# A page softmax in fewer steps through PSUM, and the substitution steps of a delta net on GpSimd: a hybrid decoder step on one NeuronCore

## The chip, the cores and the metric

The kernel runs on one core of a Trainium2 chip. Its time is the device time of one execution in microseconds (us), and a kernel's time is the median of its runs. The engines are TensorE (PE in the profile; its weight loads are PEld), VectorE (DVE), ScalarE (ACT), GpSimd (POOL) and SyncE (SP), which issues most of the DMAs. Each engine carries out its own instructions in a fixed order; semaphores make it wait for others.

## What is computed

One inference step of a hybrid decoder layer: a prompt of 1024 tokens and a sample group of 8 requests with one token each. One input projection feeds three groups of heads (differential attention, Mamba-2 SSD, gated delta net) and their gates; a projection of the concatenated heads closes the layer. Two parts matter here.

The sample group's attention reads 32 pages of 128 cached keys for each of its 8 requests, adds the new token itself, and takes a softmax over all of them for each of 4 heads x 2 maps, of which the second is subtracted with a weight lam:

```python
logits = jnp.einsum('bqhmd,bkhmd->bmhqk', q, k) * (DH_A ** -0.5)
logits = logits + rel_pos_bias(q_pos, k_pos, table)
p = jax.nn.softmax(logits, axis=-1)
wts = p[:, 0] - lam * p[:, 1]
return jnp.einsum('bhqk,bkhd->bqhd', wts, v)
```

The gated delta net solves, for each head and each chunk of 64 tokens, a unit lower triangular system, and then runs a chain over 16 chunks:

```python
lower = jnp.where(strict, beta[..., :, None] * kk * decay, 0.0)
sol = lax.linalg.triangular_solve(lower + eye, rhs, left_side=True, lower=True, unit_diagonal=True)
u, w = sol[..., :DV_C], sol[..., DV_C:]
...
S1, o = lax.scan(step, S0, seq_in)
```

## The kernel before

From about 70 to 850 us, TensorE works on the input projection (`proj_fm`, matmuls on line L458). Each weight tile is cut into a high half by ACT (`whi`, L155) and a low half by GpSimd (`wlo`, L201), and three products per pair are summed, so a late `wlo` stops TensorE. Three sets of these halves are in flight. Results leave through DVE: the convolution of a column group is one product and three multiply-adds into `cy` (L971, L167). The projections are cut into four segments (`CUTS = (9, 18, 30, 33)`), and beside each segment the function `drive` takes turns among three generators: the projections, the delta-net heads (`gdn_all`, four heads one after the other) and the sample group's pages (`sample_attention`). The kernel is built with a scheduler that simulates its own timeline and from this settles the order in which each engine gets its instructions. A segment's projections, its share of the heads and its share of the pages are all placed before the next segment's projections begin.

`sample_attention` goes over the requests. For each pair of key pages (`k_pages`) GpSimd multiplies the pages by the query in four products (`kt`, L842) and DVE sums them into the logits `lg` (L843). Behind a request's last pair comes `page_softmax`: the maximum over the pages on DVE (`smx`), a transpose on TensorE (L853) and a second maximum to join the partitions, a diagonal matrix of it (`sdg`, L857) spread by a matmul (L858), subtraction, exponentials on ACT, sums (`ssm`, matmul at L870), a reciprocal, and the weights `wz`. The new token's own logits, `slfb`, go the same way apart from the pages (`ses`, `wself`). The weights multiply the value pages on TensorE (`pv`, L898) while the next request's keys come in.

`gdn_head` handles one head of the delta net. It builds the triangular blocks of 32 rows, writes them to DRAM (`invd`) and reads them back as `Dm`, with one block on each partition. 31 substitution steps then invert all blocks at once:

```python
for j in range(31):
    n, m = 31 - j, j // 4 + 1
    tv = U[:, 8:16].rearrange("p a b -> p (a b)")[:, 0:m * n].rearrange("p (c i) -> p c i", i=n)
    tt(tv, bl(U[:, 0:m, j], n), bm(Dm[:, j, j + 1:32], m), ALU.mult)
    step = tt(U[:, 0:m, j + 1:32], U[:, 0:m, j + 1:32], tv, ALU.subtract)
    gstep[:] = [step.ins]
```

`bl` and `bm` repeat an operand over an axis; `tt` runs on DVE and shows as line L159, `tte("g", ...)` runs on GpSimd and shows as L164. These are 62 instructions a head, each on the result of the one ahead of it, with m*n elements per partition (8 to 76). The result goes through `invd` once more (L1151, L1154, issued by ACT) into `LT`, TensorE transposes it (L1163), and small matmuls join the blocks and run the chunks. Beside the steps `kb` (DVE) and `kN` (GpSimd, L1157) are scaled. `behind_gdn` puts the products or sums of `k_pages` that run on the steps' engine behind the last step written so far.

From 850 to about 1105 us the prompt's attention, the SSD, head 3 of the delta net and the last pages run; the output projection (L1833) closes the kernel.

Of the kernel before, what the change touches and what calls it, by code (L numbers as in the profile page):

```python
# [9 lines left out]
F32 = mybir.dt.float32  # L10
# [3 lines left out]
AF = mybir.ActivationFunctionType  # L14
# [5 lines left out]
P = 128  # L20
# [6 lines left out]
NPG = 32  # L27
# [51 lines left out]
def bl(ap, n):  # L79
    return ap.unsqueeze(len(ap.shape)).broadcast_to(list(ap.shape) + [n])  # L80


def bm(ap, n):
    return ap.unsqueeze(1).broadcast_to([ap.shape[0], n] + list(ap.shape[1:]))
# [3 lines left out]
def trunk_kernel(  # L88
# [61 lines left out]
    def small(shape, n, dt=F32, bufs=2):  # L150
        return sp.tile(shape, dt, tag=n, name=nm(n), bufs=bufs)

    def act(out, in_, func, bias=0.0, scale=1.0, accum=None):
        if accum is None:
            return S.activation(out, in_, func, bias=bias, scale=scale)  # L155
        return S.activation(out, in_, func, bias=bias, scale=scale, accum_out=accum)  # L156

    def tt(out, a, b, op):
        return V.tensor_tensor(out=out, in0=a, in1=b, op=op)  # L159
# [6 lines left out]
    def stt(out, a, s, b, op0, op1):  # L166
        return V.scalar_tensor_tensor(out=out, in0=a, scalar=s, in1=b, op0=op0, op1=op1)  # L167
# [601 lines left out]
        yield NT, 3.4  # L769


    lsg = const.tile([P, 4, 2], F32, name="lsg")
    G.memset(lsg, 1.0)
    slfb = const.tile([P, NS, 8], F32, name="slfb")
    wself = const.tile([P, NS, 4], F32, name="wself")
    wz = const.tile([P, NPG, 32], F32, name="wz")
# [58 lines left out]
    def k_pages(b, qb, lg, g):  # L835
        kt = kvp.tile([P, 2, 512], F32, tag="kt", name=nm("kt"), bufs=KB)
        for j in range(2):
            page(cache_k, b * NPG + 2 * g + j, kt[:, j, :])
        with behind_gdn():
            for j in range(2):  # L840
                for c in (slice(0, 256), slice(256, 512)):
                    G.tensor_tensor(out=kt[:, j, c], in0=kt[:, j, c], in1=qb[:, c], op=ALU.mult)  # L842
            V.tensor_reduce(out=lg[:, 2 * g:2 * g + 2, :], in_=kt.rearrange("p j (a d) -> p j a d", d=64), axis=AX.X, op=ALU.add)  # L843

    def page_softmax(b, lg):
        l31 = lg[:, NPG - 1, :].rearrange("p (h m) -> p h m", m=2)
        tt(l31, l31, bl(fb, 2), ALU.add)
        mx = small([P, 8], "smx")
        V.tensor_reduce(out=mx, in_=lg.rearrange("p g a -> p a g"), axis=AX.X, op=ALU.max)
        tt(mx, mx, slfb[:, b, :], ALU.max)  # L850

        pt = bank()
        TE.transpose(pt[0:8, 0:P], mx, ident)  # L853
        m8 = small([8, 1], "sm8")
        V.tensor_reduce(out=m8, in_=pt[0:8, 0:P], axis=AX.X, op=ALU.max)
        dg = small([8, 8], "sdg")
        V.tensor_scalar_mul(dg, ident[0:8, 0:8], m8)  # L857
        TE.matmul(pt[:, 256:264], ones[0:8, :], dg, start=True, stop=True)  # L858
        pmx = small([P, 8], "spm")
        V.tensor_copy(pmx, pt[:, 256:264])  # L860
        tt(lg, lg, bm(pmx, NPG), ALU.subtract)
        act(lg, lg, AF.Exp)
        es = small([P, 8], "ses")
        tt(es, slfb[:, b, :], pmx, ALU.subtract)
        act(es, es, AF.Exp)
        sm = small([P, 8], "ssm")
        V.tensor_reduce(out=sm, in_=lg.rearrange("p g a -> p a g"), axis=AX.X, op=ALU.add)
        tot = small([P, 8], "sto")
        pt = bank()
        TE.matmul(pt[:, 0:8], ones, sm, start=True, stop=True)  # L870
        tt(tot, pt[:, 0:8], es, ALU.add)
        V.reciprocal(tot, tot)
        tt(tot, tot, lsg.rearrange("p h m -> p (h m)"), ALU.mult)
        tt(lg, lg, bm(tot, NPG), ALU.mult)
        l4 = lg.rearrange("p g (h m) -> p g h m", m=2)
        if b > 0:
            G.memset(wz[:, :, 4 * b - 4:4 * b], 0.0)
        tt(wz[:, :, 4 * b:4 * b + 4], l4[:, :, :, 0], l4[:, :, :, 1], ALU.add)
        tt(es, es, tot, ALU.mult)
        e2 = es.rearrange("p (h m) -> p h m", m=2)  # L880
        tt(wself[:, b, :], e2[:, :, 0], e2[:, :, 1], ALU.add)

    vq = []

# [20 lines left out]
    def sample_attention():  # L905
        for b in range(NS + 1):
            if b < NS:
                qb = half(n="qb")
                SP.dma_start(out=qb, in_=qd[b:b + 1, :].broadcast_to([P, 512]))
                lg = small([P, NPG, 8], "lg")  # L910
            vg = 0
            for g in range(NPG // 2):
                if b < NS:
                    k_pages(b, qb, lg, g)
                    yield 2.4
                if b > 0:
                    want = 16 if b == NS else max(0, g - 2) * 16 // 13 + 1
                    while vg < min(16, g + VB if b == NS else want + 1):
                        if len(vq) == VB:
                            v_mul()  # L920
                            yield 1.0
                        v_load(b - 1, vg)
                        vg += 1
                    while len(vq) > 1 and vg - len(vq) + 1 < want and g > 2:
                        v_mul()
                        yield 1.0
            while vq:
                v_mul()
                yield 1.0
            if b < NS:  # L930
                page_softmax(b, lg)
                yield 4.0
        wd = small([NS, NS, 4], "wd", bufs=1)
        tt(wd, wself[0:NS], bl(ident[0:NS, 0:NS], 4), ALU.mult)
        TE.matmul(pv[0:32, :], wd, vS, start=False, stop=True)
        hm = small([P, 4], "hm", bufs=1)
        V.tensor_reduce(out=hm, in_=ident.rearrange("p (a h) -> p h a", h=4), axis=AX.X, op=ALU.add)
        sb = small([P, NS], "sb", bufs=1)
        V.tensor_reduce(out=sb, in_=ident.rearrange("p (j b h) -> p b j h", b=NS, h=4), axis=AX.XY, op=ALU.add)
        pvs = half(n="pvs")  # L940
        tt(pvs.rearrange("p (h d) -> p h d", d=P), pv.rearrange("p (h d) -> p h d", d=P), bl(hm, P), ALU.mult)
        pst = bank()
        TE.matmul(pst[0:NS, :], sb, pvs, start=True, stop=True)
        oS = half([NS, 512], n="oS")
        S.copy(oS, pst[0:NS, :])
        finish_sample(oS, 0)
        yield 1.0
# [94 lines left out]
    def gdn_head(h):  # L1042
# [100 lines left out]
        for j in range(31):  # L1143
            n, m = 31 - j, j // 4 + 1
            tv = U[:, 8:16].rearrange("p a b -> p (a b)")[:, 0:m * n].rearrange("p (c i) -> p c i", i=n)
            tt(tv, bl(U[:, 0:m, j], n), bm(Dm[:, j, j + 1:32], m), ALU.mult)
            step = tt(U[:, 0:m, j + 1:32], U[:, 0:m, j + 1:32], tv, ALU.subtract)
            gstep[:] = [step.ins]
            yield 0.5
        for g in range(4):  # L1150
# [533 lines left out]
    fb = const.tile([P, 4], F32, name="fb")  # L1684
    V.tensor_copy(fb, pst[:, 0:4])

    V.tensor_copy(lsg[:, :, 1], nlam.broadcast_to([P, 4]))

    sample_q()
    smp = sample_attention()  # L1690
    drive((chain(items(1), small_cols()), 52.0), (take(smp, 16 * 2.4 - 0.1), 40.0))
# [252 lines left out]
```

## Time and profile before

| | before |
|---|---|
| runs, us | 1272.66, 1275.63, 1278.05; median 1275.63 |
| profiled execution, us | 1270.58, span 1268.8 |
| TensorE busy | 1136.3 us, mean granted clock 0.947 of full speed |
| DVE busy | 833.6 us |
| GpSimd busy | 643.8 us |
| ACT busy | 471.6 us |

The span is the time from the first to the last instruction in the trace of the profiled execution. The share of busy time is a mean over stretches that have different limits; what ends an engine's idle time in a stretch is read from the waits and the rows in time. The granted clock is 1 at 2.4 GHz and 0.5 at 1.2 GHz.

### The profile page before, as it was taken

How to read it: one execution, taken by the hardware profiler on the slowest of the kernel's cores; microseconds unless marked ns; L12 is line 12 of the kernel's file. 1: busy time of each engine (PE TensorE's matmuls, PEld its weight loads, DVE VectorE, ACT ScalarE, POOL GpSimd, SP SyncE). 2: the span in 40 equal slices, each digit the busy share in tenths (PEclk: the TensorE clock that was granted, in tenths of full speed). 3: DMA queues.
4: the chain of work that ended last, by engine and by line, in shares of the span. 5: the costliest groups of instructions: out<-in, count | busy, mean ns of one | idle time of the engine just before them, and what ended most of it. 6: DMA issues, size and time to landing. Idle time of an engine off the chain costs nothing.

```text
span 1268.8 us, 22346 instructions
## 1 busy us (share of the span) xinstructions
PE 1136.3 (90%) x7365; PEld 959.4 (76%) x7365; DVE 833.6 (66%) x1994; ACT 471.6 (37%) x998; POOL 643.8 (51%) x779
## 2 busy tenths in 40 slices
PE   4999999989889988888997799988899999799997
PEld 3799887768669777867866688866568778678876
DVE  6723698549478658945754955787878988664444
ACT  6332223211114332233353233436737759341111
POOL 3747867646665653573965778772023251341100
PEclk9999999989789988898988899998998999899999
DMA  8646765994884962696797599999786664961420
GB/s 298 200 164 205 238 208 161 349 324 134 280 293 155 319 214 77 190 333 211 234 318 226 183 322 336 307 287 257 219 225 174 161 167 133 299 198 52 131 69 34
DMA packets 246452, 275.57 MB, mean 217 GB/s; under 512 B 31905, under 2 KB 163376, under 8 KB 246322
## 3 DMA queue, kind: packets, MB, share of 16 engines
q1 hardware_dynamic: 168082, 214.44, 52.3%
q10 hardware_dynamic: 78256, 59.72, 16.4%
q8 instruction: 58, 0.95, 0.3%
q14 instruction: 56, 0.46, 0.1%
HBM read 231.59 MB, written 42.67 MB: 216 GB/s over the span
## 4 chain that ended last, share of the span: by engine, by line
PE 53%; DMA 16%; DVE 15%; issue 5%; ACT 3%; SPq 3%; POOL 3%; ACTq 1%; DVEq 0%; POOLq 0%
PE b L458 23%; PE b L1833 10%; PE pv L898 4%; DMA kt<-in_cache_k_dram 3%; DVE U L159 3%; DMA vt<-in_cache_v_dram 3%; DMA w<-in_w_in_dram 2%; DVE lg L843 2%; DVE cy L167 2%; PE b L745 1%; SPq L823 1%; POOL kt L842 1%; PE b L1893 1%; DVE e L721 1%; DMA zb<-zfd 1%
## 5 line engine op out<-in xcount | busy, mean ns | idle before, releaser
L458 PE MATMUL b<-hh,whi 128*128 128x344 f32 (+1 forms) x2016 | 508.6, 335 | 23.0 <-DVE cy L167 11.6
L842 POOL TENSOR_TENSOR kt<-kt,qb 128x256 f32<-128x256 f32 x512 | 364.5, 745 | 159.8 <-DMA kt<-in_cache_k_dram 104.0
L458 PEld LDWEIGHTS b<-hh,whi 128*128 128x128 f32 x2016 | 363.7, 197 | 56.0 <-issue 30.1
L458 PE MATMUL b<-hh,wlo 128*128 128x344 f32 (+1 forms) x1008 | 332.4, 334 | 3.5 <-POOL wlo L201 3.5
L843 DVE TENSOR_REDUCE lg<-kt 128x16 f32<-128x1024 f32 x128 | 154.6, 1211 | 88.0 <-POOL kt L842 85.2
L458 PEld LDWEIGHTS b<-hh,wlo 128*128 128x128 f32 x1008 | 197.1, 196 | 15.7 <-issue 10.1
L201 POOL TENSOR_TENSOR wlo<-w,whi 128x512 fp32r<-128x512 f32 x86 | 111.1, 1297 | 92.9 <-ACT whi L155 80.5
L1833 PE MATMUL b<-wo,mh 128*128 128x512 f32 (+1 forms) x408 | 121.7, 380 | 0.2 <-POOL wo L1567 0.2
L155 ACT ACTIVATE whi<-w 128x512 fp32r<-128x512 f32 x86 | 54.1, 631 | 160.8 <-PE b L458 114.4
L167 DVE SCALAR_TENSOR_TENSOR cy<-b,vec,cy 128x341 f32<-128x341 f32 (+4 forms) x180 | 99.0, 563 | 1.5 <-DVE U L159 0.2
L898 PE MATMUL pv<-vt,wz 128*32 128x512 f32 x512 | 78.3, 645 | 22.6 <-DMA vt<-in_cache_v_dram 15.0
L1833 PEld LDWEIGHTS b<-wo,mh 128*128 128x128 f32 x408 | 74.6, 188 | 14.5 <-POOL wo L1567 0.4
L1833 PE MATMUL b<-wo,ml 128*128 128x512 f32 (+1 forms) x204 | 77.1, 378 | 0.0
L1801 POOL TENSOR_TENSOR ml<-zt,mh 128x512 fp32r<-128x512 f32 x16 | 22.4, 1404 | 104.7 <-ACT mh L1800 104.5
L159 DVE TENSOR_TENSOR U<-U,Dm 128x60 f32<-128x60 f32 (+24 forms) x124 | 40.6, 327 | 18.7 <-DMA Dm<-invd 16.8
L156 ACT ACTIVATE e<-e,nmx 128x128 f32<-128x128 f32 (+7 forms) x64 | 48.9, 766 | 8.8 <-DVE nmx L723 5.4
L155 ACT ACT_TABLE_LOAD x33 | 42.3, 1283 | 25.5 <-DMA qh<-qfd 8.5
L718 PE MATMUL b<-kTh,qh 128*128 128x128 f32 (+3 forms) x96 | 41.1, 431 | 11.7 <-DVE mx L721 6.5
L159 DVE TENSOR_TENSOR y<-b,gate 128x512 f32<-128x512 f32 (+1 forms) x17 | 11.1, 658 | 54.2 <-PE b L1833 54.2
L1833 PEld LDWEIGHTS b<-wo,ml 128*128 128x128 f32 x204 | 38.3, 188 | 7.3
L971 DVE TENSOR_SCALAR cy<-b,vec 128x344 f32<-128x344 f32 (+1 forms) x60 | 33.2, 564 | 14.5 <-PE b L458 14.3
L898 PEld LDWEIGHTS pv<-vt,wz 128*32 128x32 f32 x512 | 12.4, 110 | 39.6 <-issue 18.9
(531 smaller groups left out, 2022.9 us busy)
## 6 DMA issues: line engine op xcount, KB each, us to landing
kt<-in_cache_k_dram SPq DMA_DIRECT2D x256, 256.0 KB
vt<-in_cache_v_dram SPq DMA_DIRECT2D x256, 256.0 KB
w<-in_w_in_dram ACTq DMA_DIRECT2D x82, 256.0 KB
zfd<-zf ACTq DMA_DIRECT2D x12, 512.0 KB
wo<-in_w_out_dram SPq DMA_DIRECT2D x12, 512.0 KB
om<-mixd SPq DMA_DIRECT2D x24, 256.0 KB
xt<-in_x_prompt_dram SPq DMA_DIRECT2D x8, 512.0 KB
hx<-in_w_ada_dram SPq DMA_DIRECT2D x16, 256.0 KB
```

The costliest lines, as they stand in the source:

```text
L155: return S.activation(out, in_, func, bias=bias, scale=scale)
L156: return S.activation(out, in_, func, bias=bias, scale=scale, accum_out=accum)
L159: return V.tensor_tensor(out=out, in0=a, in1=b, op=op)
L167: return V.scalar_tensor_tensor(out=out, in0=a, scalar=s, in1=b, op0=op0, op1=op1)
L201: G.tensor_tensor(out=lo, in0=w32, in1=hi.bitcast(F32), op=ALU.subtract)
L458: TE.matmul(ps[:, 0:N], a, b[k][:, sl], start=(i == 0), stop=(i == 23))
L718: TE.matmul(ps[:, 0:b - a], qh[:, m, ts], kT[m][:, a:b], start=True, stop=False)
L842: G.tensor_tensor(out=kt[:, j, c], in0=kt[:, j, c], in1=qb[:, c], op=ALU.mult)
L843: V.tensor_reduce(out=lg[:, 2 * g:2 * g + 2, :], in_=kt.rearrange("p j (a d) -> p j a d", d=64), axis=AX.X, op=ALU.add)
L898: mm = TE.matmul(pv[32 * r:32 * r + 32, :], wz[:, 2 * g + j, :], vt[:, j, :], start=(b == 0 and g < 2), stop=(b == NS - 1 and g >= 14 and ...
L971: V.tensor_scalar_mul(y[:, c0_:c0_ + m], ps[:, o:o + m], wv[3])
L1833: TE.matmul(ps[c], m[a][:, kt % 4, :], w[kt][:, c[0]:c[1]], start=(kt == KT[0] and i == 0), stop=(kt == KT[-1] and i == 2))
```

## The change

Two parts. In `page_softmax` the new token's logits become row 32 of `lg`, copied there by ACT, so that maximum, exponential, normalisation and the subtraction of the second map handle pages and new token together. The diagonal matrix, the copy of the spread maximum out of PSUM and the separate steps on `ses` go; DVE reads the spread maximum and the reciprocal from PSUM directly, and the factor -lam moves into the last two instructions, so `lsg` goes too. The pairs of key pages are visited in the order 14, 15, 0, 1, ..., 13, and the bias of the last page is added behind the second pair. In `gdn_head` the 62 substitution steps of a head move from DVE to GpSimd. `behind_gdn` then orders GpSimd's `kt` products behind the steps, where it ordered DVE's sums.

```diff
     def page_softmax(b, lg):
-        l31 = lg[:, NPG - 1, :].rearrange("p (h m) -> p h m", m=2)
-        tt(l31, l31, bl(fb, 2), ALU.add)
+
+        if b == 0:
+            S.copy(lg[:, NPG, :], slfb[:, b, :])
         mx = small([P, 8], "smx")
         V.tensor_reduce(out=mx, in_=lg.rearrange("p g a -> p a g"), axis=AX.X, op=ALU.max)
-        tt(mx, mx, slfb[:, b, :], ALU.max)
...
-        dg = small([8, 8], "sdg")
-        V.tensor_scalar_mul(dg, ident[0:8, 0:8], m8)
-        TE.matmul(pt[:, 256:264], ones[0:8, :], dg, start=True, stop=True)
-        pmx = small([P, 8], "spm")
-        V.tensor_copy(pmx, pt[:, 256:264])
-        tt(lg, lg, bm(pmx, NPG), ALU.subtract)
+        TE.matmul(pt[:, 256:264], m8.broadcast_to([8, P]), ident[0:8, 0:8], start=True, stop=True)
+        tt(lg, lg, bm(pt[:, 256:264], NPG + 1), ALU.subtract)
         act(lg, lg, AF.Exp)
-        es = small([P, 8], "ses")
-        tt(es, slfb[:, b, :], pmx, ALU.subtract)
-        act(es, es, AF.Exp)
         sm = small([P, 8], "ssm")
-        V.tensor_reduce(out=sm, in_=lg.rearrange("p g a -> p a g"), axis=AX.X, op=ALU.add)
-        tot = small([P, 8], "sto")
+        V.tensor_reduce(out=sm, in_=lg[:, 0:NPG].rearrange("p g a -> p a g"), axis=AX.X, op=ALU.add)
         pt = bank()
         TE.matmul(pt[:, 0:8], ones, sm, start=True, stop=True)
-        tt(tot, pt[:, 0:8], es, ALU.add)
-        V.reciprocal(tot, tot)
-        tt(tot, tot, lsg.rearrange("p h m -> p (h m)"), ALU.mult)
-        tt(lg, lg, bm(tot, NPG), ALU.mult)
+        tot = small([P, 8], "sto")
+        tt(tot, pt[:, 0:8], lg[:, NPG, :], ALU.add)
+        V.reciprocal(pt[:, 8:16], tot)
+        tt(lg, lg, bm(pt[:, 8:16], NPG + 1), ALU.mult)
...
-        tt(wz[:, :, 4 * b:4 * b + 4], l4[:, :, :, 0], l4[:, :, :, 1], ALU.add)
-        tt(es, es, tot, ALU.mult)
-        e2 = es.rearrange("p (h m) -> p h m", m=2)
-        tt(wself[:, b, :], e2[:, :, 0], e2[:, :, 1], ALU.add)
+        stt(wz[:, :, 4 * b:4 * b + 4], l4[:, 0:NPG, :, 1], nlam, l4[:, 0:NPG, :, 0], ALU.mult, ALU.add)
+        stt(wself[:, b, :], l4[:, NPG, :, 1], nlam, l4[:, NPG, :, 0], ALU.mult, ALU.add)
...
-                    k_pages(b, qb, lg, g)
+                    k_pages(b, qb, lg, (g - 2) % (NPG // 2))
+                    if g == 1:
+                        l31 = lg[:, NPG - 1, :].rearrange("p (h m) -> p h m", m=2)
+                        tt(l31, l31, bl(fb, 2), ALU.add)
...
-            tt(tv, bl(U[:, 0:m, j], n), bm(Dm[:, j, j + 1:32], m), ALU.mult)
-            step = tt(U[:, 0:m, j + 1:32], U[:, 0:m, j + 1:32], tv, ALU.subtract)
+            tte("g", tv, bl(U[:, 0:m, j], n), bm(Dm[:, j, j + 1:32], m), ALU.mult)
+            step = tte("g", U[:, 0:m, j + 1:32], U[:, 0:m, j + 1:32], tv, ALU.subtract)
```

Lines behind the diff have numbers lower by 7 in the kernel of the change (L1163 is L1156 there, L1151 is L1144, L1157 is L1150), L842 is L840 and L898 is L886. The order of the instructions changes with it. Two places follow.

First place: GpSimd, in the substitution steps of head 0. Before, GpSimd has here weight splits (`wlo`), page products (`kt`) and `kN`:

```order
L201 TENSOR_TENSOR wlo_3659<-w_473_3624,whi_3658 128x512
L842 TENSOR_TENSOR kt_3439<-kt_3439,qb_3265 128x256 x4
L201 TENSOR_TENSOR wlo_3746<-w_474_3626,whi_3745 128x512
L842 TENSOR_TENSOR kt_3500<-kt_3500,qb_3265 128x256 x4
L201 TENSOR_TENSOR wlo_3912<-w_502_3877,whi_3911 128x512
```

With the change the steps (`U_2827`; the ones with `Dm` are the products, the others the differences) stand among them, here near their end:

```order
L201 TENSOR_TENSOR wlo_3727<-w_468_3607,whi_3726 128x512
L164 TENSOR_TENSOR U_2827<-U_2827 128x6x8
L201 TENSOR_TENSOR wlo_3893<-w_496_3858,whi_3892 128x512
L164 TENSOR_TENSOR U_2827<-U_2827,Dm_2822 128x49
L164 TENSOR_TENSOR U_2827<-U_2827 128x7x7
L164 TENSOR_TENSOR U_2827<-U_2827,Dm_2822 128x42
L164 TENSOR_TENSOR U_2827<-U_2827 128x7x6
L164 TENSOR_TENSOR U_2827<-U_2827,Dm_2822 128x35
L164 TENSOR_TENSOR U_2827<-U_2827 128x7x5
L840 TENSOR_TENSOR kt_3337<-kt_3337,qb_3244 128x256 x4
L164 TENSOR_TENSOR U_2827<-U_2827,Dm_2822 128x28
```

The split `wlo_3893` is the last one ahead of the end of head 0's steps; 15 steps and 4 `kt` products stand behind it up to the last step.

Second place: TensorE, at the transpose of head 2's `LT`. Before, it stands among the projections of the segment that ends at item 30 (`b`, L458), with 68 of them still to come:

```order
L458 MATMUL b_8566<-hh_514,wlo_8393 128x344
L458 MATMUL b_8566<-hh_525,whi_8392 128x344
L1163 MATMUL b_8155<-ident,LT_7281 128x128 x4
L1163 MATMUL b_8163<-ident,LT_7281 128x128 x4
L898 MATMUL pv<-vt_8396,wz 32x512 x2
L898 MATMUL pv<-vt_8408,wz 32x512 x2
L458 MATMUL b_8566<-hh_526,whi_8392 128x344
L458 MATMUL b_8566<-hh_525,wlo_8393 128x344
```

With the change:

```order
L458 MATMUL b_8666<-hh_772,whi_8422 128x344
L458 MATMUL b_8666<-hh_771,wlo_8423 128x344
L886 MATMUL pv<-vt_8021,wz 32x512 x2
L886 MATMUL pv<-vt_8089,wz 32x512 x2
L886 MATMUL pv<-vt_8167,wz 32x512 x2
L886 MATMUL pv<-vt_8283,wz 32x512 x2
L1156 MATMUL b_8100<-ident,LT_7235 128x128 x4
L1156 MATMUL b_8108<-ident,LT_7235 128x128 x4
L1168 MATMUL b_8147<-T_958_7426,LT_7235 32x32 x4
L1169 MATMUL b_8148<-T_958_7426,LT_7235 32x32 x4
```

The transpose moved behind the last projection of its segment (`b_8666`). Between the segment's last projection and the next segment's first one stand 104 other matmuls, those on pages (`pv`) included; before there were 36.

## Rows read from the trace of the kernel before

**Rows 1.** The page, part 1: busy us, share of span, instructions.
```profile
PE 1136.3 (90%) x7365; PEld 959.4 (76%) x7365; DVE 833.6 (66%) x1994; ACT 471.6 (37%) x998; POOL 643.8 (51%) x779
```

**Rows 2.** TensorE's waits: line, releaser, us in total, times, longest.
```profile
PE b L858 <- DVE sdg L857: 4.1, 2, 3.6
PE pv L898 <- DVE wz L159: 4.0, 2, 2.8
...
PE b L458 <- POOL wlo L201: 3.5, 3, 2.7
```

**Rows 3.** TensorE in time, four windows: start, us, instruction, [idle before].
```profile
482.23 0.94 PE L458 MATMUL b<-hh,whi 128*128 128x344 f32 x2 [6.14 <-DVE cy L167]
...
700.24 0.27 PE L853 MATMUL b<-ident,smx 128*8 128x128 f32 x1 [2.02 <-DVE U L159]
...
709.59 0.59 PE L858 MATMUL b<-sdg,ones 8*128 8x8 f32 x2 [3.62 <-DVE sdg L857]
...
727.45 1.08 PE L898 MATMUL pv<-vt,wz 128*32 128x512 f32 x8 [2.78 <-DVE wz L159]
```

**Rows 4.** Windows: busy us of PE, PEld, DVE, ACT, POOL; PEclk; DMA.
```profile
559.50:578.90 19.40, 13.81 (x106) 8.90 (x105) 13.56 (x23) 3.57 (x7) 16.07 (x23) 0.89 0.95 312
688.00:731.40 43.40, 34.99 (x189) 33.29 (x188) 41.43 (x98) 10.64 (x17) 27.94 (x33) 0.85 0.56 178
731.40:766.30 34.90, 34.90 (x303) 29.91 (x301) 14.19 (x16) 13.53 (x26) 26.27 (x33) 0.99 0.98 321
...
900.00:940.00 40.00, 35.44 (x242) 22.39 (x242) 34.29 (x162) 16.35 (x47) 4.54 (x8) 1.00 0.82 241
```

**Rows 5.** Windows of instructions on tile U: DVE busy, POOL busy, PEclk, DMA.
```profile
276.00:321.40 45.40, 17.61 (x62) 0.00 (x0) 1.00 0.64 201
...
688.00:731.40 43.40, 25.82 (x62) 0.00 (x0) 0.85 0.56 178
...
900.00:940.00 40.00, 14.78 (x62) 0.00 (x0) 1.00 0.82 241
```

**Rows 6.** Rows in time on TensorE at the ends of two segments.
```profile
334.20 1.06 PE L1163 MATMUL b<-ident,LT 128*128 128x128 f32 x8 [1.83 <-DMA LT<-invd]
...
774.10 0.56 PE L458 MATMUL b<-hh,whi 128*128 128x344 f32 x2
...
775.13 0.48 PE L458 MATMUL b<-hh,whi 128*128 128x344 f32 x2
```

**Rows 7.** GpSimd by line and form: busy us, mean ns, idle before.
```profile
L842 POOL TENSOR_TENSOR kt<-kt,qb 128x256 f32<-128x256 f32 x512 | 364.5, 745 | 159.8 <-DMA kt<-in_cache_k_dram 104.0 <-DVE U L159 12.8 <-DMA qb<-qd 10.7
L201 POOL TENSOR_TENSOR wlo<-w,whi 128x512 fp32r<-128x512 f32 x86 | 111.1, 1297 | 92.9 <-ACT whi L155 80.5 <-PE b L1119 9.7 <-PE b L458 1.4
...
L164 POOL TENSOR_TENSOR stm<-sst,sbc 128x256 f32<-128x256 f32 x8 | 7.8, 994 | 6.4 <-DVE sst L159 6.4
L1157 POOL TENSOR_TENSOR kN<-kN,fkd 128x1024 f32<-128x1024 f32 x4 | 7.6, 1897 | 10.9 <-DVE kb L159 10.9
```

**Rows 8.** Rows in time on GpSimd: a memset and the copies behind it.
```profile
946.51 0.31 POOL L1497 MEMSET gwz<- 128x256 f32 x1 [2.11 <-PE b L1501]
946.88 0.33 POOL L1499 COPY gwz<-gWQ 128x8 f32<-128x8 f32 x2
```

**Rows 9.** Rows in time: steps on DVE alone, then beside GpSimd's kt products.
```profile
483.33 0.19 DVE L159 TENSOR_TENSOR U<-U,Dm 128x30 f32<-128x30 f32 x1
483.56 0.19 DVE L159 TENSOR_TENSOR U<-U 128x30 f32<-128x30 f32 x1
...
698.67 3.54 POOL L842 TENSOR_TENSOR kt<-kt,qb 128x256 f32<-128x256 f32 x5 [3.06 <-DMA qb<-qd]
...
700.26 0.64 DVE L159 TENSOR_TENSOR U<-U,Dm 128x63 f32<-128x63 f32 x1
```

**Rows 10.** Tile U: count, ns min/median/max, first and last start.
```profile
L159 DVE TENSOR_TENSOR U<-U,Dm x124: 156/211/1826, 276.2 to 938.9; 128x60 f32<-128x60 f32 x12, 128x28 f32<-128x28 f32 x8, 128x54 f32<-128x54 f32 x8, 128x48 f32<-128x48 f32 x8
```

**Rows 11.** DVE by line and form: a product that GpSimd runs too.
```profile
L164 DVE TENSOR_TENSOR stm<-sst,sbc 128x256 f32<-128x256 f32 x8 | 6.0, 766 | 0.0
```

More of the change, by code (lines that the diff above doesn't have):

```diff
@@ L769, in attn_head @@
         yield NT, 3.4
-    lsg = const.tile([P, 4, 2], F32, name="lsg")
-    G.memset(lsg, 1.0)
     slfb = const.tile([P, NS, 8], F32, name="slfb")
@@ L909, in sample_attention @@
                 SP.dma_start(out=qb, in_=qd[b:b + 1, :].broadcast_to([P, 512]))
-                lg = small([P, NPG, 8], "lg")
+                lg = small([P, NPG + 1, 8], "lg")
+                if b > 0:
+                    S.copy(lg[:, NPG, :], slfb[:, b, :])
             vg = 0
@@ L1685, in trunk_kernel @@
     V.tensor_copy(fb, pst[:, 0:4])
-    V.tensor_copy(lsg[:, :, 1], nlam.broadcast_to([P, 4]))
     sample_q()
```

## The prediction

> **What bounds the kernel now.** I read the page's shares of the engines first: TensorE is busy for 90% of the span, DVE for 66%, GpSimd for 51% [rows 1]. So the change pays only where TensorE waits for DVE, and costs only where TensorE comes to wait for GpSimd. Next come TensorE's own waits. The page softmax's maximum (sdg) and weights (wz) hold it for 4.1 and 4.0 us in two places each [rows 2]. The rows in time show the largest of these, and a wait of the softmax's transpose, within one stretch: 2.02, 3.62 and 2.78 us [rows 3]. It is the stretch in which the third delta-net head (head 2) runs its 62 substitution steps on DVE. DVE is busy there for 41.43 of 43.40 us, and TensorE's mean granted clock is 0.85 [rows 4]. With the two levels of 2.4 and 1.2 GHz that is 30% of the stretch at the lower one, so some 6.5 us of matmul time went with the clock, and 8.4 us with the three waits. A fourth wait, of 6.14 us, stands at the start of head 1's steps and ends with a convolution sink on DVE [rows 3].
>
> Each head is also a chain: 62 dependent steps, two trips through DRAM (invd, LT), a transpose on TensorE (L1163), and a row of small matmuls behind it. The windows over tile U give the steps 17.61, 25.82 and 14.78 us of DVE at heads 0, 2 and 3, inside stretches of 45, 43 and 40 us [rows 5]. Where a segment's projections run out, TensorE has little besides this chain. At head 0 it waited 1.83 us until LT had landed at 334.20 [rows 6], 12.8 us after the steps' end near 321.4. At head 1 the last part of the delta net took 19.4 us, with TensorE busy for 13.81 [rows 4]. Head 2 escaped that: projections go on at 774.10 [rows 6], behind a part in which TensorE was never idle (731.4 to 766.3, rows 4).
>
> **The price of a step on GpSimd.** The trace of before has no U step there. The nearest rows are products and differences of two f32 operands: 745 ns at 256 elements, 1297 ns at 512 [rows 7]. The line through them is 193 ns + 2.16 ns an element. A head's 31 products and 31 differences have 1560 elements each (the sum of m*n in the code), so 62 x 0.193 + 3120 x 0.00216 = 18.7 us. Each step also waits for the one ahead of it: a GpSimd copy that needs a memset starts at 946.88, the memset ends at 946.51 + 0.31 [rows 8], so 60 ns, 3.7 us a head. Together **22.4 us a head, 0.36 us a step**. On DVE a step of 30 elements takes 0.19 us and the next starts 0.23 us after it, but 0.64 us beside GpSimd's kt products [rows 9]; that is how head 2 came to its 25.82 us. My lower bound is DVE's undisturbed pace, 62 x 0.23 = 14.3 us. The upper is 0.5 us a step, twice the foot of the line with its wait (2 x 0.253), 31 us. I take the line, since 8 to 76 elements lie near its foot.
>
> That DVE's steps grow beside kt products is what the Trainium skill ("SBUF — State Buffer", Who interferes with whom) has for a DVE instruction with two SBUF inputs against a GpSimd instruction that reads SBUF: one blocks the other for a whole instruction. The trace agrees, 0.64 against 0.19 us. By that rule the moved steps would go on holding up DVE's two-input work, for a third of a microsecond at a time.
>
> **Part by part.**
> - *Softmax.* DVE loses some ten short instructions per sample, eight times. TensorE's waits for sdg, wz and the transpose are about 10 us, 8.4 of them in head 2's stretch, which has its own term. Elsewhere **-2** (0 to -5). ACT gains a copy of 8 elements per sample, at a use of 37% [rows 1]; I cost it at nothing, because ACT cuts weights several matmuls ahead of their use, and where that lead is gone it costs its own 0.2 us, eight times.
> - *Head 0.* In the order of the change GpSimd has 62 steps, 16 kt products, 6 weight splits and kN in one row: 22.4 + 16 x 0.745 + 6 x 1.297 + 1.9 = 44.0 us. From 276.2 that ends at 320.2, as before, if nothing waits. But the last split (wlo_3893) stands ahead of the last 15 steps and 4 kt products, and 54 projection matmuls ahead of the segment's end. At about 0.17 us each (six in 1.03 us, rows 6) with some page matmuls between them that is near 321. Then 1.3 + 15 x 0.3 + 3.0 us put the chain's end near 329, and LT at 341 against 334.2, or 3 us sooner where the split's high half is ready sooner: **+5** (-1.6 to +10).
> - *Head 1.* Sinks no longer queue with steps, so the wait of 6.14 us and the half clock behind it should shrink. The steps still start when Dm has landed. **-3** (0 to -8).
> - *Head 2.* The largest term. In the order of before the transpose stands 68 projections ahead of the segment's end; in the order of the change it stands behind all of them, and 104 other matmuls, those on pages included, are left with no projection among them, where it was 36. GpSimd's row within the chain is 62 steps, 20 kt products, 8 splits, 12 products of the sample state (at most 0.994 us each) and kN: 22.4 + 14.9 + 10.4 + 11.9 + 1.9 = 61.5 us [rows 7]. From 688.1 that is 749.6; the trips, 12 to 12.8 us as at head 0, bring 762. The serial part takes at least the 19.4 us that head 1's took, so projections resume near 783 against 774.10: **+9**. TensorE's vanished waits (8.4 + 6.5 us) and the moved matmuls bring it to the segment's end sooner, near 740, and are swallowed by the wait for LT. Low, at DVE's pace: 688.1 + 14.3 + 39.1 + 12 + 19.4 = 772.9, -1. High, at 0.5 us a step: 758 + 12.8 + 22 = 793, +19.
> - *Head 3.* GpSimd is nearly empty there (4.54 us of 40), DVE has 34.29, TensorE 35.44 [rows 4]. 14.78 us leave DVE, and TensorE's 4.6 us of idle time bound the gain: **-3** (0 to -4.6). The chain itself, 22.4 us with little between its steps, fits its old 40 us.
> - *Given back.* Where TensorE is later, page transfers are further ahead of it: **-2**.
>
> Sum: -2 + 5 - 3 + 9 - 3 - 2 = +4 us. The profiled execution took 1270.58 us (span 1268.8), 5 us less than the median of the three runs, so 1274.6 for such an execution and **1279.5 us** for a median of runs. A measurement tells 0.5%, 6.4 us, from no change; +4 is inside that. By itself this case spans 1269 to 1282.
>
> **The rivals.**
> - *The relief comes through: faster, 1257.* If steps cost DVE's pace on GpSimd, or fill the time in which GpSimd waited for kt pages (104 us in all, rows 7), heads 0 and 2 give -1.6 and -1, head 1 -8, softmax -5, head 3 -3: -19 us. For it: DVE's 41.43 of 43.40 us, and GpSimd at 26.27 of 34.9 us beside a TensorE that never idles [rows 4]. Against: 61 us of work in one row ahead of head 2's transpose. It decides where a step costs under 0.27 us.
> - *Late weight splits: slower, 1294.* Twenty splits now queue among steps and kt products. In the order of before the first matmul on such a split stands 14 to 60 projections behind it; in that of the change, five have 7 to 11, or 1.2 to 1.9 us. If GpSimd lags the planned order by more, TensorE stalls by the lag: at 0.46 us a step 62 x 0.1 = 6 us a head, over three heads +18. Against: TensorE waited for splits for 3.5 us in all [rows 2], and the planned spacing of 2.4 to 2.75 projections a step, 0.41 to 0.47 us, is wider than my price. It decides from about 0.45 us a step.
> - *Steps at twice DVE's duration: slower, 1288.* DVE's products of a step have a median of 211 ns [rows 10]. Twice that, 62 x 0.422 = 26.2 us a head, is 4 us over my price, and heads 0 and 2 both end that much later: +8. The Trainium skill ("GPSIMD Engine Reference", Engine selection) has GpSimd about twice as slow for elementwise work on two inputs. This trace shows 994 ns on GpSimd [rows 7] against 766 ns on DVE [rows 11] for the same 256-element product, a ratio of 1.3, so it bears the rule out only in part.
> - *Hidden anyway.* Both parts concern engines off the path and the transposes come in time: 1272 to 1276, within the likeliest case's span.
>
> **How the numbers follow.** No measurable change 0.37, relief 0.27, late splits 0.20, twice the duration 0.12, slower in other ways 0.04: faster 0.27, same 0.37, slower 0.36. The range runs from the relief's 1257, less 1 us, to the late splits' 1294 plus 3; it leaves out about half of the first and a third of the second.
>
> **What would show it.** Right: U steps on GpSimd near 0.30 us with gaps near 60 ns; hardly any idle time on GpSimd from head 2's first step to its last; L1156 of head 2 waiting for LT, projections resuming near 783; head 0's LT near 340; no softmax wait of TensorE over 1 us elsewhere. Wrong: steps under 0.25 or over 0.43 us, TensorE waiting for wlo by over 10 us in sum, or head 2's LT landing before TensorE reaches the segment's end.

## The result, and the profile after

The change makes the kernel slower: a median of 1292.93 us (1290.80 to 1297.42, 4 runs) against 1276.84 us (4 runs), a ratio of 1.0139 with a 95% interval of 1.0103 to 1.0174. The profiled execution, of 1297.42 us, is the slowest of the four, so some 4 us of its span are not in the median. Where runs of one kernel lie over 1.5% above its fastest, as two of the four of experiment 7 do, they are given apart and no median is taken over them.

The engines' shares in the page of the change, beside [rows 1]:

```profile
PE 1150.5 (89%) x7365; PEld 969.4 (75%) x7365; DVE 765.3 (59%) x1697; ACT 477.0 (37%) x1002; POOL 712.0 (55%) x1026
```

DVE has 68 us less to do, GpSimd 68 us more, and TensorE's share falls by a point. TensorE's waits in the change (line, releaser, us in total, times, longest), beside [rows 2]:

```profile
PE pv L886 <- DMA vt<-in_cache_v_dram: 21.0, 8, 8.7
PE b L1218 <- ACT oC L155: 11.1, 3, 5.6
PE b L458 <- POOL wlo L201: 9.6, 4, 3.8
...
PE b L458 <- DVE cy L167: 6.7, 4, 3.0
...
PE b L1156 <- DMA LT<-invd: 5.4, 2, 4.9
...
PE pv L886 <- DVE wz L167: 0.4, 1, 0.4
```

Of the softmax's waits of 4.1 and 4.0 us (for `sdg` and `wz`) 0.4 us are left. In their place stand longer waits for value pages (21.0 us against 15.0 before, among them one of 8.7), for the chunk chain of the delta net (11.1, `oC`) and for `LT` (5.4). The waits for splits are 9.6 us against 3.5.

The substitution steps, beside [rows 10] and [rows 5], first their durations (ns, min/median/max), then windows from each head's first step to its last, for tile U alone (GpSimd's busy us, PEclk, DMA):

```profile
L164 POOL TENSOR_TENSOR U<-U,Dm x124: 203/290/1318, 278.1 to 940.9; 128x60 f32<-128x60 f32 x12, 128x28 f32<-128x28 f32 x8, 128x54 f32<-128x54 f32 x8, 128x48 f32<-128x48 f32 x8
L164 POOL TENSOR_TENSOR U<-U x124: 211/292/1104, 278.4 to 941.2; 128x60 f32<-128x60 f32 x12, 128x28 f32<-128x28 f32 x8, 128x54 f32<-128x54 f32 x8, 128x48 f32<-128x48 f32 x8
```

```profile
278.00:324.70 46.70, 17.54 (x62) 1.00 0.56 176
484.20:529.50 45.30, 18.31 (x62) 0.99 0.40 125
685.20:744.40 59.20, 19.91 (x62) 0.97 0.55 165
916.70:941.50 24.80, 19.02 (x62) 0.88 0.84 254
```

The medians are 290 and 292 ns. At head 3, where GpSimd runs little else, 62 steps take 24.8 us with 19.02 us busy; without one other product of 1.0 us that is 0.38 us a step. At head 2 they fill only 19.91 of 59.2 us.

TensorE in time at the transposes of heads 0 and 2, at the next segment's first projection, and at a wait in the last segment, beside [rows 6]:

```profile
335.48 0.87 PE L1156 MATMUL b<-ident,LT 128*128 128x128 f32 x3 [4.89 <-DMA LT<-invd]
...
755.53 1.93 PE L886 MATMUL pv<-vt,wz 128*32 128x512 f32 x8 [8.69 <-DMA vt<-in_cache_v_dram]
757.40 0.90 PE L1156 MATMUL b<-ident,LT 128*128 128x128 f32 x3
...
779.83 0.59 PE L458 MATMUL b<-hh,whi 128*128 128x344 f32 x2
...
807.73 0.58 PE L1218 MATMUL b<-vn,kN 128*128 128x128 f32 x1 [5.58 <-ACT oC L155]
```

Head 0's `LT` lands at 335.48. Head 2's transpose runs at 757.40, behind a page matmul that waited 8.69 us, and projections go on at 779.83. Counted from the first projection matmul of the kernel, TensorE had issued number 2688 of 3048 at 745.53, against 766.10 before: it came to the segment's end 20.6 us sooner and left it 5.7 us later.

Four stages by that count show where the time goes. Each number is the distance in us between the starts of two projection matmuls of one profiled execution: 1009 to 1177 ends with head 0's transpose and chain, 1177 to 1537 is the first part of the segment behind it, 2353 to 2689 covers head 2's steps and its chain, 2689 to 3048 is the last segment.

| kernel | 1009 to 1177 | 1177 to 1537 | 2353 to 2689 | 2689 to 3048 |
|---|---|---|---|---|
| before | 72.0 | 85.6 | 85.5 | 73.0 |
| the change | 76.2 | 85.9 | 94.9 | 82.8 |
| softmax part alone (twice) | 75.3, 76.1 | 82.0, 82.0 | 86.6, 85.3 | 74.7, 73.9 |
| head 2 back on DVE | 77.4 | 86.6 | 85.1 | 74.6 |
| head 2 alone on GpSimd | 75.0 | 84.5 | 96.4 | 82.3 |
| head 0 alone on GpSimd | 75.1 | 86.8 | 93.1 | 74.8 |
| old softmax, steps on GpSimd (2) | 78.4 | 87.1 | 93.0 | 79.8 |
| half the page products, steps on DVE (5) | 66.9 | 89.6 | 91.4 | 84.7 |
| half the page products, steps on GpSimd (6) | 67.3 | 86.5 | 91.8 | 84.0 |
| state products and `kN` on DVE (7) | 67.3 | 83.6 | 87.2 | 77.5 |

Against the kernel before, the change loses 4.2 us in head 0's stage, 9.4 us in head 2's and 9.8 us in the last segment. It gains 7.4 us between 1537 and 2353 (227.6 against 235.0 us), and 11 us more go behind the projections, of which the last section speaks.

### The profile page after: what moved, and what is told of

Same layout as the page of the kernel before. It is cut to its first block, busy times and chain, and to the rows that moved or that the text cites. A ratio compares the mean times of both kernels' runs of the same rounds, so it can differ in the third digit from the quotient of the medians.

```text
span 1295.7 us, 22265 instructions
## 1 busy us (share of the span) xinstructions
PE 1150.5 (89%) x7365; PEld 969.4 (75%) x7365; DVE 765.3 (59%) x1697; ACT 477.0 (37%) x1002; POOL 712.0 (55%) x1026
## 4 chain that ended last, share of the span: by engine, by line
PE 50%; DMA 20%; DVE 11%; POOL 8%; issue 5%; ACT 2%; SPq 2%; ACTq 1%; POOLq 0%; DVEq 0%
PE b L458 21%; PE b L1824 10%; PE pv L886 4%; POOL kt L840 4%; DMA vt<-in_cache_v_dram 3%; DMA kt<-in_cache_k_dram 3%; DMA w<-in_w_in_dram 3%; POOL U L164 2%; POOL wlo L201 1%; DMA Y<-yxd 1%; DVE lg L841 1%; DVE e L721 1%; PE b L745 1%; DMA om<-mixd 1%; SPq L821 1%
## 5 line engine op out<-in xcount | busy, mean ns | idle before, releaser
L458 PE MATMUL b<-hh,whi 128*128 128x344 f32 (+1 forms) x2016 | 503.9, 333 | 13.4 <-DVE cy L167 6.7
L840 POOL TENSOR_TENSOR kt<-kt,qb 128x256 f32<-128x256 f32 x512 | 362.3, 742 | 98.9 <-DMA kt<-in_cache_k_dram 77.8
L458 PEld LDWEIGHTS b<-hh,whi 128*128 128x128 f32 x2016 | 359.9, 195 | 45.7 <-issue 24.5
L458 PE MATMUL b<-hh,wlo 128*128 128x344 f32 (+1 forms) x1008 | 330.3, 332 | 9.6 <-POOL wlo L201 9.6
L458 PEld LDWEIGHTS b<-hh,wlo 128*128 128x128 f32 x1008 | 195.2, 194 | 19.8 <-POOL wlo L201 10.9
L886 PE MATMUL pv<-vt,wz 128*32 128x512 f32 x512 | 82.0, 682 | 25.3 <-DMA vt<-in_cache_v_dram 21.0
L1824 PEld LDWEIGHTS b<-wo,mh 128*128 128x128 f32 x408 | 74.7, 188 | 14.1
L164 POOL TENSOR_TENSOR U<-U,Dm 128x60 f32<-128x60 f32 (+24 forms) x124 | 38.3, 309 | 43.8 <-DMA Dm<-invd 36.5
L156 ACT ACTIVATE e<-e,nmx 128x128 f32<-128x128 f32 (+7 forms) x64 | 49.1, 768 | 6.7 <-DVE nmx L723 3.4
L721 DVE CUSTOM_DVE_ANT_0 e<-b,bt 128x512 f32<-128x512 f32 (+3 forms) x64 | 37.1, 583 | 12.3 <-PE b L719 10.8
L886 PEld LDWEIGHTS pv<-vt,wz 128*32 128x32 f32 x512 | 12.0, 113 | 41.5 <-issue 14.9
```

Source lines behind the costliest of these rows:

```text
L164: return EN[e].tensor_tensor(out=out, in0=a, in1=b, op=op)
L458: TE.matmul(ps[:, 0:N], a, b[k][:, sl], start=(i == 0), stop=(i == 23))
L721: V.tensor_tensor_reduce(out=e[m][:, a:b], in0=ps[:, 0:b - a], in1=bias, scale=1.0, scalar=-3.0e38, op0=ALU.add, op1=ALU.max, accum_out=mx ...
L886: mm = TE.matmul(pv[32 * r:32 * r + 32, :], wz[:, 2 * g + j, :], vt[:, j, :], start=(b == 0 and g < 2), stop=(b == NS - 1 and g >= 14 and ...
L1824: TE.matmul(ps[c], m[a][:, kt % 4, :], w[kt][:, c[0]:c[1]], start=(kt == KT[0] and i == 0), stop=(kt == KT[-1] and i == 2))
```

## The experiments

Theory A: chains on GpSimd end late at segment ends, above all head 2's. A1 has this come from sharing GpSimd's one row with page products and splits, A2 from the order alone. Theory B: late weight splits stop TensorE. Theory C: the softmax part, its page order or any new order costs the time. Theory D: DVE and GpSimd hold each other up wherever both work. Edits are against the change unless said otherwise.

**1. Softmax part alone.** Steps back on DVE at all heads:

```diff
-            tte("g", tv, bl(U[:, 0:m, j], n), bm(Dm[:, j, j + 1:32], m), ALU.mult)
-            step = tte("g", U[:, 0:m, j + 1:32], U[:, 0:m, j + 1:32], tv, ALU.subtract)
+            tt(tv, bl(U[:, 0:m, j], n), bm(Dm[:, j, j + 1:32], m), ALU.mult)
+            step = tt(U[:, 0:m, j + 1:32], U[:, 0:m, j + 1:32], tv, ALU.subtract)
```

> The softmax part and its page order alone; all 62 steps of every head stay on DVE. Theory A (the loss comes from chains on GpSimd that end behind the last projection of a segment, above all head 2's): the softmax part is a gain of some 4 to 10 us, so 1266 to 1273 us. Theory B (the loss comes from late weight splits on GpSimd): the same, since the splits do not queue with steps here. Theory C (the loss comes from the softmax part, its page order, or from any re-planning): 1283 us or more, and the steps' move is worth nothing.

Measured: 1267.82 us, ratio 0.9948 (0.9921 to 0.9974). C falls: by itself the softmax part, with its page order, is a gain. Whether the order that comes with the moved steps costs time is A2's question.

**2. Steps alone.** The four lines of the steps in the kernel before, its softmax untouched.

> The steps of all four heads on GpSimd, the softmax as before. Theory A: head 2's transpose again stands behind the segment's last projection with 104 matmuls after it, so about as slow as the whole change or slower, 1290 to 1300 us. Theory B: the same. Theory C: 1270 to 1280 us.

Measured: 1289.78 us, ratio 1.0124 (1.0082 to 1.0165). So the steps make the loss. With the steps on GpSimd the softmax part gains nothing that can be measured (the change has 1.0103 to 1.0174), though alone it gains 0.5 to 0.8%. Where that gain goes was not shown: beside this kernel the change is 1.9 us slower in head 2's stage and 3.0 us in the last segment, yet 6.2 us ahead at matmul 3048 (862.61 against 868.78 us), and behind all the same at the end (spans of 1295.7 and 1290.3 us).

**3. Head 2 back on DVE.**

```diff
+            e = "g" if h in (0, 1, 3) else "v"
-            tte("g", tv, bl(U[:, 0:m, j], n), bm(Dm[:, j, j + 1:32], m), ALU.mult)
+            tte(e, tv, bl(U[:, 0:m, j], n), bm(Dm[:, j, j + 1:32], m), ALU.mult)
...
```

> The whole change, with the steps of head 2 alone back on DVE; the order up to head 2 is that of the change. Theory A: the transpose of head 2 comes back among projections (48 of them behind it, 44 matmuls at the segment's end instead of 104), projections resume some 10 us sooner than in the change, so 1278 to 1284 us. Theory B (late splits): a third of the loss goes, 1287 us. Theory C: no difference from the change, 1290 to 1295 us.

Measured: 1278.67 us, ratio 1.0027 (0.9995 to 1.0059). One head gives back 14 us, as A said. TensorE in time at head 2's transpose and at the next segment's first projection:

```profile
752.96 0.71 PE L1157 MATMUL b<-ident,LT 128*128 128x128 f32 x5
...
774.30 0.56 PE L458 MATMUL b<-hh,whi 128*128 128x344 f32 x2
```

The transpose stands among projections without a wait, and head 2's stage (85.1 us) and the last segment (74.6 us) are as short as with the softmax part alone.

**4. Head 3 alone on GpSimd.** The same edit with `(3,)`.

> The softmax part with the steps of head 3 alone on GpSimd; heads 0 to 2 on DVE. Against the softmax alone of the same job this prices head 3. My step of the prediction: -3 us (0 to -4.6). Rival: the profile of the change lost some 11 us behind the last projection; if head 3's place on GpSimd made that loss, this run is 6 to 11 us above the softmax alone.

Measured: 1272.49 us, ratio 1.0003 (0.9969 to 1.0037), so 5 us over the softmax part alone. The expected gain is not there; the two intervals touch, so how large the loss is stays rough, and its place was not found (see the last section). The chain itself is sooner: in this profile head 3's transpose runs at 947.7 us, in the two of the softmax part alone at 956.6 and 965.4. So a sooner chain is not what that stretch lacked.

**5 and 6. Half of the page products left out**, once with the steps on DVE, once with the change's:

```diff
-                for c in (slice(0, 256), slice(256, 512)):
+                for c in (slice(0, 256),):
                     G.tensor_tensor(out=kt[:, j, c], in0=kt[:, j, c], in1=qb[:, c], op=ALU.mult)
```

> Softmax part, steps on DVE, and half of the kt products left out (the second 256 columns of each page are not multiplied by the query), so that GpSimd has some 180 us less to do. Partner of the next run; by itself, with the page products hidden as they are, about as the softmax part alone, 1262 to 1270 us.

> The whole change with the same half of the kt products left out. Theory A1 (the steps cost time because they share GpSimd's one row with kt products and splits, so that chains end late and page products pile up behind them): with 10 to 15 us less of other work in each chain, head 2's chain ends some 7 us sooner, the piled-up products go, and the distance to the partner falls from 25 us to under 10. Theory A2 (the steps cost time by the order alone: transposes that stand behind the segment's last projection with about 100 matmuls and no projection after them): the order still has head 2's transpose there, with 100 matmuls, so the distance stays at 12 us or more.

Measured: 1264.04 us (ratio 0.9890, 0.9833 to 0.9947) and 1271.62 us (0.9933, 0.9902 to 0.9963). The distance between steps on GpSimd and on DVE falls from 25 us to 7.6 us, with head 2's transpose still behind the segment's last projection. That is what A1 forecast, but the intervals overlap, and their far ends (0.9833 and 0.9963) are over 16 us apart, so A2's 12 us are not excluded.

The stages settle it no better. Head 2's stage and the last segment take 91.4 and 84.7 us with the steps on DVE, 91.8 and 84.0 us with them on GpSimd. There is no difference between the two kernels, but both are as slow there as the change (94.9 and 82.8), and the softmax part alone is not (86.6 and 74.7). The partner loses this time although head 2's steps are on DVE and its transpose stands among projections, with 47 still to come in the segment; it even has a wait for the delta net's `oC` in the last segment, as the change has:

```profile
730.63 1.04 PE L1156 MATMUL b<-ident,LT 128*128 128x128 f32 x8
...
798.60 0.80 PE L1218 MATMUL b<-vn,kN 128*128 128x128 f32 x2 [5.43 <-ACT oC L155]
```

Why it loses it with less work on GpSimd is open. So A1 fits the totals, but these two runs neither show it nor refute A2: a long row on GpSimd and the order that follows from it stay together.

**7. Sample-state products and kN on DVE.**

```diff
-                G.tensor_tensor(out=st[:, b], in0=st[:, b], in1=bl(ex[:, 1, :, 2 * q + b], P), op=ALU.mult)
+                V.tensor_tensor(out=st[:, b], in0=st[:, b], in1=bl(ex[:, 1, :, 2 * q + b], P), op=ALU.mult)
...
-                    tte("gv"[g], tmp[:, 2 * g:2 * g + 2, :], bm(bc[:, g, b, :], 2), bl(xdt[:, 2 * g:2 * g + 2, 2 * q + b], P), ALU.mult)
+                    tte("v", tmp[:, 2 * g:2 * g + 2, :], bm(bc[:, g, b, :], 2), bl(xdt[:, 2 * g:2 * g + 2, 2 * q + b], P), ALU.mult)
...
-        G.tensor_tensor(out=kN, in0=kN, in1=bl(fkd, P), op=ALU.mult)
+        V.tensor_tensor(out=kN, in0=kN, in1=bl(fkd, P), op=ALU.mult)
```

> The whole change, with the sample-state products (sst, stm) and kN moved from GpSimd to DVE: 12 to 14 us less in GpSimd's row inside head 2's chain, 2 us less in the other heads' chains. The order puts head 2's steps at projections 2348 to 2598 (2688 in the change) and its transpose 31 projections ahead of the segment's end. Theory A: LT lands some 12 us sooner, the loss at head 2 falls by 8 us or more, 1281 to 1286 us. Theory B (late splits) and theory D (DVE and GpSimd hold each other up wherever both work): 1290 us or more.

A second line of `stm` products, not shown, moves likewise. Measured: 1264.93 and 1265.74 us in two runs, 1285.64 and 1287.50 us in two more; the kernel before, run beside it, had 1280.28 us. The profile is of the run of 1264.93 us. Head 2's steps in a window from first to last, tile U alone:

```profile
663.60:712.70 49.10, 23.51 (x62) 0.93 0.57 168
```

With other work gone from GpSimd's row, the steps take 49.1 us from first to last instead of 59.2. The first two runs lie 15 us under the kernel before, and 16 us under what A forecast at the least, so more than A's price went with this edit, and what more is open. The other two are at the upper end of A's range and just above it. No run reaches the 1290 us of B and D. But D's effect is there, in a smaller size: the busy time of the steps rose from 19.91 to 23.51 us, and the longest of them, of 2.41, 1.44 and 1.21 us, run beside products on DVE. And as the transpose comes back among projections here, this run, too, does not tell A1 from A2.

**8. Head 1 alone on GpSimd.** The edit of 3 with `(1,)`.

> The softmax part with the steps of head 1 alone on GpSimd, the one head whose chain does not end at a segment's last projection and has few page products behind it. My step of the prediction for head 1 was -3 us against the steps on DVE, so 1263 to 1267 us, and the best kernel of this study. If GpSimd loses wherever it takes steps: 1270 us or more.

Measured: 1262.13 us, ratio 0.9859 (0.9806 to 0.9912): the fastest kernel of this study. It is 6 us under the softmax part alone by medians not taken side by side, with an interval that overlaps the second of that kernel's two (0.9887 to 0.9945, below).

**9 to 12. One job on a common base:** the softmax part again; head 0 alone, `(0,)`; head 2 alone, `(2,)`; and the softmax part with the pages in their old order:

```diff
-                    k_pages(b, qb, lg, (g - 2) % (NPG // 2))
-                    if g == 1:
+                    k_pages(b, qb, lg, g)
+                    if g == NPG // 2 - 1:
```

> The softmax part alone again, as the common base of this job: a ratio of 0.99 to 0.995 to the kernel before, as the first time (0.9948).

> The softmax part with the steps of head 0 alone on GpSimd. Prediction's term for head 0: +5 us. From the profiles of the change and of the softmax part alone, the part behind head 0's transpose took 36 us instead of 28, with ten more us of kt products in it, so theory A1 (chain and piled-up page products) gives +6 to +10 us over the base. If only chain ends count (LT landed at the same time in both), 0 to +2 us.

> The softmax part with the steps of head 2 alone on GpSimd; its transpose stands behind the segment's last projection with 104 matmuls after it, as in the change. Prediction's term: +9 us, swallowing TensorE's vanished waits. From the run with head 2 put back, +14 us against the base. If head 2's loss came only together with what heads 0 and 1 had done to the order: under +5 us.

> The softmax part alone with the key pages in their old order 0 to 15 and the bias of the last page added behind the last pair. If the gain of the softmax part comes from its shorter chain between the last page and the weights, it stays, within 3 us of the base; if it comes from the page order (the last page's bias off the chain), most of it goes, 5 us or more over the base.

| kernel | median us | ratio to before, interval |
|---|---|---|
| softmax part again | 1268.18 | 0.9916 (0.9887 to 0.9945) |
| head 0 alone | 1278.36 | 1.0014 (0.9981 to 1.0047) |
| head 2 alone | 1291.61 | 1.0100 (1.0047 to 1.0154) |
| softmax part, old page order | 1276.21 | 0.9990 (0.9957 to 1.0023) |

Head 0 costs 10 us alone, head 2 23 us. The four heads' single prices (10, -6, 23 and 5) add up to 32 us, while the change costs 25 us more than the softmax part alone, so they are not independent of one another. Without the page order the softmax part is worth nothing that can be measured; 8 us of its gain come with the order of the pages and the place of the last page's bias. Which of these two, or the new order of instructions that follows from them, was not tried.

Head 2 alone, TensorE in time: the page matmul ahead of the transpose, the transpose, the next segment's first projection, and the wait in the last segment:

```profile
751.28 1.93 PE L886 MATMUL pv<-vt,wz 128*32 128x512 f32 x8 [8.42 <-DMA LT<-invd]
753.29 1.08 PE L1157 MATMUL b<-ident,LT 128*128 128x128 f32 x4
...
776.65 0.58 PE L458 MATMUL b<-hh,whi 128*128 128x344 f32 x2
...
804.27 0.79 PE L1219 MATMUL b<-vn,kN 128*128 128x128 f32 x2 [4.98 <-ACT oC L155]
```

The picture of the change comes back with this one head: a wait of 8.42 us at the segment's end and one of 4.98 us for a chunk of the delta net in the last segment. The profile puts the first down to `LT` here and to a value page in the change. The matmul that waits reads value pages; transfers of both kinds are under way in both runs, so this does not tell which of the two held TensorE.

## Why the prediction was right or wrong

The forecast was 1279.5 us in a range of 1256 to 1297; measured were 1292.93 us, inside the range, but with a loss of 16 us where 4 were forecast. The case called likeliest, no measurable change, did not happen; the loss of 1.4% lies between the rivals "twice the duration" and "late splits", and neither of their mechanisms made it. That the range reaches so far is owed to late splits (1294), so that the number lies inside it is luck. What is right is the mechanism at head 2. Wrong in size are the terms for head 2, which stopped at the segment's end, for head 0 and for the softmax; wrong in sign are those for head 3 and for what page transfers were to give back.

- **The price of a step: right.** It was 0.30 us plus a wait of 0.06. Medians are 0.29 us, the busy sums 17.5 to 19.9 us a head against 18.7, and 0.38 us a step from start to start at head 3 against 0.36. So the rival with twice DVE's duration falls: doubling 211 ns would have been 422 ns. That doubling is what the Trainium skill ("GPSIMD Engine Reference", Engine selection) states for two-input work; at 8 to 76 elements these runs show 290 against 211 ns, a ratio of 1.4.
- **Head 2's chain: right.** GpSimd was to have 61.5 us of work from the first step to the last; it took 59.2 us, with GpSimd busy for 55.66 of them (windows below). Projections were to resume near 783, after an arrival of TensorE near 740; they resumed at 779.83 after an arrival at 745.53. The stage lost 9.4 us against +9. The sign that `L1156` would wait for `LT` did not come by that name: the wait of 8.69 us stands ahead of it, on a page matmul. The relief is real as well: during the steps TensorE is busy for 55.52 of 59.20 us at a clock of 0.97, in the two profiles of the softmax part alone for 34.76 and 34.21 of 42.00 us at 0.92 and 0.96, and waits it off behind.
- **Head 2's term: half of it missing.** The sum let everything be as before once projections had resumed. The last segment lost 9.8 us more: 4.9 us of idle time, and 4.9 us in which about as many matmuls take longer (TensorE is busy for 77.10 of 82.78 us at a clock of 0.96, before for 72.19 of 73.01 us at 1.00). With all page products this loss stands where head 2 is on GpSimd (the change, head 2 alone, old softmax with the steps) and not where it is on DVE. But it also stands in experiment 5, with head 2 on DVE and half of the products, so head 2 on GpSimd is not the only way to it. What TensorE waits for is the head's chain of chunks, which runs in this segment in every kernel here (its first matmul on `kN` starts at 780.6 us before and at 783.7 us in the change) and in the change meets other work on ACT. ACT in time in the change, up to the chunk's copy `oC` that TensorE waited 5.58 us for:

```profile
799.44 4.28 ACTq L647 DMA_DIRECT2D ql<-qfd  x2
803.76 0.45 ACT L991 COPY zf<-b 128x344 f32<-128x344 f32 x1 [6.63 <-DMA ql<-qfd]
...
805.07 1.28 ACT L155 ACT_TABLE_LOAD   x1
806.36 1.06 ACT L155 ACTIVATE zf<-zf 128x1032 f32<-128x1032 f32 x1
807.33 0.35 ACT L155 ACTIVATE oC<-b,f 128x128 f32<-128x128 f32 x1
```

ACT computes nothing for 6.63 us, in which it issues loads for the prompt's attention (4.28 us for the two `ql` alone), then has a table load and `zf` ahead of `oC`. Behind the stall the clock falls too: the mean grant from 800 to 816 us is 0.79, against 1.00 in the softmax part alone. That this stall makes the whole 9.8 us was not shown.
- **Head 0: near by number, wrong by place, and too small alone.** The term laid the loss to a late `LT`, at 341. `LT` landed at 335.48, 1.3 us later than before, and TensorE came to the segment's end 4.1 us sooner. The stage lost 4.2 us all the same (against +5), about half of it behind the transpose: from there to the next segment's projections it takes 35.9 us (335.48 to 371.41), 33.8 before, and 28.2 and 28.9 in the softmax part alone. Windows of all engines (PE, PEld, DVE, ACT, POOL, then PEclk, DMA's share and GB/s) in the change, from the first segment's end to the next one's first projection, and over head 2's steps:

```profile
328.20:371.40 43.20, 28.18 (x217) 17.54 (x216) 20.97 (x31) 6.92 (x18) 31.19 (x44) 0.62 0.85 284
685.20:744.40 59.20, 55.52 (x341) 53.61 (x340) 24.00 (x36) 22.36 (x32) 55.66 (x104) 0.97 0.55 165
```

and the same two stretches of the softmax part alone:

```profile
329.70:363.50 33.80, 24.01 (x206) 15.73 (x205) 15.35 (x24) 7.52 (x19) 20.93 (x29) 0.70 0.91 298
677.30:719.30 42.00, 34.76 (x209) 32.30 (x207) 39.95 (x92) 10.64 (x17) 27.24 (x31) 0.92 0.60 177
```

From the last step to the next segment's projections GpSimd has 32.28 us of page products in the change, 27.41 before and 20.68 in the softmax part alone, and TensorE's page matmuls wait 4.9 us for value pages from 325 to 372 us, against 0.3 in the softmax part alone. I had counted the page products ahead of the last step, not those pushed behind it. That these are the cause was not shown.

Alone this head costs 10 us (against +5), and not at its own place: its first stage is as in the softmax part alone (75.1 against 75.3 and 76.1). 4.8 us go in the segment behind, and 6.5 to 7.8 us in head 2's stage (93.1 against 86.6 and 85.3), though head 2's steps are on DVE in both. There TensorE waits again for the softmax, in this run for 10.4 us, in the two of the softmax part alone for 5.7 and 5.4 us:

```profile
693.55 0.37 PE L851 MATMUL b<-ident,smx 128*8 128x128 f32 x1 [3.36 <-DVE U L164]
...
701.92 0.38 PE L854 MATMUL b<-ident,sm 8*128 8x8 f32 x2 [3.42 <-DVE sm L853]
...
717.21 1.93 PE L886 MATMUL pv<-vt,wz 128*32 128x512 f32 x8 [3.65 <-DVE wz L167]
```

So a part of head 0's price comes from what its move does to a later stage. Whether through the order or through the time at which pages are ready was not tried.
- **Head 1: sign right,** -3 against -6 measured. Its transpose does not stand at a segment's end.
- **Head 3: wrong.** -3 was expected from DVE's relief, +5 measured. The chain came sooner (4. above) and the kernel did not, so TensorE's idle time there was not the steps' to give back; what takes the 5 us is open.
- **Given back: wrong.** -2 was expected because page transfers would be further ahead. TensorE waits for value pages for 21.0 us against 15.0 before, and 8.9 and 7.3 in the softmax part alone.
- **Softmax elsewhere: too small,** -2 against -7 to -10 for the part alone. Its stalls at head 2 were thought to be swallowed by the chain; that head 2's stage is no shorter in the change than with the old softmax (94.9 against 93.0 us, 2. above) agrees with it. But most of the gain of the part alone hangs on the page order and the place of the last page's bias, which the prediction did not price at all. The part also takes some six DVE instructions per sample away (49 in all besides the 248 steps), not ten.
- **Late splits (B): falls.** The sign against the forecast, over 10 us of waits for `wlo`, was missed by little. But 6.6 of the 9.6 us lie ahead of the first step at 278, where the change moves no step. Within a head's steps there is one:

```profile
698.78 0.43 PE L458 MATMUL b<-hh,wlo 128*128 128x344 f32 x1 [2.98 <-POOL wlo L201]
```

## What to carry to other kernels

Work moved to an idle engine may be paid where that engine's one row has to be finished before another engine may go on: here 62 steps of 19.91 us took 59.2 us, since GpSimd's row was 56 of 59 us full. A mean use of 51% says nothing about such a stretch. So add up everything queued ahead of the last moved instruction, and look also at what it pushes behind itself and at the stages that follow: 9.8 us of the change's loss stand in a segment in which it moves no step. Where a moved part is made of several like pieces, move them one at a time: here head 1 costs nothing (6 us less by medians), while heads 0, 2 and 3 cost 10, 23 and some 5 us, and the prices do not add up.

## What was not expected

- Two executions of one kernel (the softmax part) agree to 0.2 us at the end of the projections (838.97 and 839.12 for matmul 3048) and end with spans of 1262.9 and 1273.4 us. So the 11 us that the profile of the change loses behind the projections can't be laid to the change from one profile, and head 3's price rests on medians alone.
- The order in which a request's key pages are visited, together with the place of the last page's bias, is worth 8 us with the same products and transfers (0.9916 against 0.9990, intervals apart).
